# Turning x once and ordering the first projection block by hand in an SSD and attention trunk

## The chip, the core and the metric

The kernel runs on one core of a Trainium2 chip. The metric is the device time of one launch in microseconds. A core has TensorE (PE; the profile shows its weight loads apart, as PEld), VectorE (DVE), ScalarE (ACT), GpSimd (POOL) and SyncE (SP), which here only issues transfers. Each engine works through its own instructions in order; semaphores tie the engines together. ACT and POOL issue some transfers too, in order with their own work.

## The reference, cut to what matters

Sixteen meta tokens are put ahead of 1024 tokens of 1024 features; so L is 1040. Layer 0 is an SSD (Mamba-2) mixer and a gated FFN, layer 1 an attention and a gated FFN. The change lies at the very start of layer 0: the norm of the input, the first projections, and dt.

```python
def _rmsnorm(x, g):
    y = x32 * lax.rsqrt(jnp.mean(x32 * x32, axis=-1, keepdims=True) + NORM_EPS)
    return (y * g.astype(jnp.float32)).astype(x.dtype)

def _ssd_mixer(u, w_in, conv_w, conv_b, dt_bias, a_log, d_skip, gate_g, w_out):
    z, xbc, dt_raw = jnp.split(u @ w_in, [SSM_D_INNER, SSM_D_INNER + SSM_CONV_DIM], axis=-1)
    xbc = jax.nn.silu(_causal_dwconv(xbc, conv_w, conv_b))
    xs, b_in, c_in = jnp.split(xbc, [SSM_D_INNER, SSM_D_INNER + G * N], axis=-1)
    dt = jax.nn.softplus(dt_raw.astype(f32) + dt_bias.astype(f32))
    a = -jnp.exp(a_log.astype(f32))
...
    a_cs = jnp.cumsum(jnp.transpose(dt_c * a.reshape(G, E), (0, 3, 4, 1, 2)), axis=-1)
    decay_in = jnp.exp(jnp.where(causal, a_cs[..., :, None] - a_cs[..., None, :], -jnp.inf))
...
# per layer: h = h + mixer(rmsnorm(h)); h = h + ffn(rmsnorm(h))
```

## The kernel before

**Layout.** The stream h and the operands stand with features on the 128 partitions (eight tiles of 128 features, `KD = 8`) and tokens along the free axis. Tokens are cut into nine chunks of 116 (`CH`; the last has 112) and into three token tiles `TT` of 348, 348 and 344, three chunks each. x arrives with tokens on the partitions and has to be turned by PE, a 116 x 128 piece at a time, against the identity.

**Products.** A projection is made in three products of rounded numbers (`mm3`, lines 151 to 153): weights and operand are each split into a high part (a copy of ACT to the type fp32r) and a low part (the difference), and high x high, high x low and low x high are summed in PSUM. A block is 128 output features; for one token tile it takes 8 x 3 = 24 products (`project`). `load_w` fetches a block's weights on SP's queue, ACT makes the high part (line 144), POOL the low part (line 145).

**The start, `load_x`.** Nine chunks of x are fetched in turn on the queues of ACT and SP (`by_rows`, line 357). For each token tile j there are two steps, put in the order `ORD`:
- `stream(j)`: sums of squares of each token (line 318 on ACT, line 316 on DVE); for each k three turns (line 323), a copy to h (lines 326 and 328), and one fp32 product of `w_dt`, scaled by the norm's gain beforehand, with h for dt (line 329); then the token factors r (`token_rstd`, lines 202 to 208). For j = 2 each h is also spilled to memory (line 331).
- `scaled(j)`: x is multiplied by r in place, a token to a partition (line 340), turned a second time (line 345), and split with the gain into the operands `uh` and `ul` (lines 256 and 257).

**dt, `dt_path`.** A generator of three stages. The first takes the raw dt sums, turns them to tokens on partitions (line 403), multiplies by r (line 412), adds the bias and forms softplus. The second takes the running sums of dt*a within a chunk (lines 432 and 433). The third turns them back (line 445) and writes them to memory as `acs_d` and `ea_d` (line 451), from which the scan fetches them spread over partitions as D (line 567) and E (line 573).

**Group 0.** `mixer` then runs the six blocks of group 0 (`in_group`), each with three token tiles: project, a convolution of four taps (line 273 on ACT, three times line 276 on DVE), and silu (line 464), which `settle` leaves until the next convolution. A stage of `dt_path` is run after tiles 2, 5 and 8. PSUM gives the projections two banks (`mm`), and one more (`ex`) to each third tile. Then comes the scan of group 0, between whose steps the blocks of later groups are put; the scan's first products are lines 594 and 597, and its first DVE work on D is line 578.

**What sets the order.** Outside of `manual_schedule` the compiler's scheduler orders each engine's instructions after its own model of their times, and may put a later instruction ahead of an earlier one that isn't ready. Inside `manual_schedule` the instructions of PE, DVE, ACT and POOL keep the order of the program among themselves; others may still be put between them. SP's transfers are left to the scheduler. Before the change `load_x` and the six blocks of group 0 are ordered by the scheduler; the scan and all after it in the mixer by hand.

Of the kernel before, what the change touches and what calls it, by code (L numbers as in the profile page):

```python
# [8 lines left out]
F32 = mybir.dt.float32  # L9
# [4 lines left out]
P = 128  # L14
# [35 lines left out]
ORD = ((0, 0), (1, 0), (0, 1), (1, 1), (0, 2), (1, 2))  # L50
XB, SQD = 9, (1, 4, 7)
# [15 lines left out]
class Trunk:  # L67
    def __init__(self, ctx, tc, a):
# [10 lines left out]
        self.open = []  # L79
        self.consts()  # L80
# [198 lines left out]
    def load_x(self, pool, mx):  # L279
# [5 lines left out]
        wdt = self.wp.tile([P, 1024], F32, tag="w32", name="wdt")  # L285
        self.ln_exp()
        d = self.dp.tile([KD, P, L], F32, tag="h0_d", name="h0_d")
        r9 = mx.tile([P, 3, 3], F32, tag="r9", name="r9")
        dt = self.ex("dtr")
        xs = []  # L290
        for c, (t0, n) in enumerate(CH):
            xt = pool.tile([P, D], F32, tag="x", name=self.nm("x"), bufs=XB)
            if c == 0:
                nc.sync.dma_start(xt[:META, :], a["meta"])
                self.by_rows(nc.scalar, xt[META:n, :], a["x"][: n - META, :], n - META)
            else:
                self.by_rows(nc.sync if c % 2 else nc.scalar, xt[:n, :], a["x"][t0 - META : t0 - META + n, :], n)
            if c == 0:
# [3 lines left out]
            xs.append(xt)  # L302
        u = [(self.Q("uh", F32R), self.Q("ul", F32R)) for _ in range(KD)]
# [4 lines left out]
        def stream(j):  # L308
            s0, nn = TT[j]
            x3 = xs[3 * j : 3 * j + 3]  # L310
            for i in range(3):
                c = 3 * j + i
                n = CH[c][1]
                t = self.wp.tile([P, D], F32, tag="wl", name=self.nm("junk"))
                if c in SQD:
                    nc.vector.scalar_tensor_tensor(t[:n, :], x3[i][:n, :], 1.0, x3[i][:n, :], op0=ALU.mult, op1=ALU.mult, accum_out=ss[:n, c : c + 1])
                else:
                    nc.scalar.activation(t[:n, :], x3[i][:n, :], AF.Square, accum_out=ss[:n, c : c + 1])
            for k in range(KD):
                ps = self.lg("xT")  # L320
                for i in range(3):
                    n = CH[3 * j + i][1]
                    nc.tensor.transpose(ps[:, i * CB : i * CB + n], x3[i][:n, k * P : k * P + P], self.ident[:n, :n])
                h = hs[k][:, s0 : s0 + nn]
                if k % 2:
                    nc.scalar.activation(h, ps[:, :nn], AF.Copy)
                else:
                    nc.vector.tensor_copy(h, ps[:, :nn])
                nc.tensor.matmul(dt[j * H : j * H + H, :nn], wdt[:, k * H : k * H + H], h, start=k == 0, stop=k == KD - 1)
                if j == 2:  # L330
                    nc.sync.dma_start(d[k], hs[k][:, :L])
            self.token_rstd(ss[:, 3 * j : 3 * j + 3], CB, 3, y=r9[:, :, j])

        def scaled(j):
            s0, nn = TT[j]
            x3 = xs[3 * j : 3 * j + 3]
            for i, t in enumerate(x3):
                n = CH[3 * j + i][1]
                r = r9[:n, i : i + 1, j]
                nc.vector.tensor_scalar(t[:n, :], t[:n, :], r, None, op0=ALU.mult)  # L340
            for k in range(KD):
                ps = self.sm("xr")
                for i in range(3):
                    n = CH[3 * j + i][1]
                    nc.tensor.transpose(ps[:, i * CB : i * CB + n], x3[i][:n, k * P : k * P + P], self.ident[:n, :n])
                self.parts(ps[:, :nn], u[k], s0, nn, self.par("ssd_norm", k))

        for step, j in ORD:
            (scaled if step else stream)(j)
        return d, u, dt, r9  # L350
# [35 lines left out]
    def dt_path(self, ps, r9, cp):  # L386
# [10 lines left out]
        rows = self.tmp("rows")  # L397
        nc.gpsimd.memset(rows[:G, TT[2][1] : 3 * CB], 0.0)
        for j, (_, n) in enumerate(TT):
            nc.scalar.activation(rows[j * H : j * H + H, :n], ps[j * H : j * H + H, :n], AF.Copy)  # L400
        pv = self.sm("dt")
        for i in range(3):
            nc.tensor.transpose(pv[:CB, i * G : i * G + G], rows[:G, i * CB : i * CB + CB], self.ident[:G, :G])
# [1162 lines left out]
```

## Time and profile before

| | |
|---|---|
| runs | 3008.25, 3008.68, 3009.84 us; median 3008.68 |
| profiled execution | 3009.7 us, of which the span of the trace is 3008.0 |
| PE busy in the span | 2886.3 us (96%) |
| PE weight loads | 2776.1 us (92%) |
| DVE, ACT, POOL busy | 2304.7, 1653.0, 1306.0 us |
| fp32 dt products (line 329), first 138 us | 21.54 us busy |
| turns of line 323 and of line 345, first 138 us | 14.43 and 11.57 us busy |

A row of the order of time gives the start in us from the start of the span, the duration, engine, line, operation, what it writes and reads, the shapes and the count; in brackets the idle time of the engine ahead of it and what ended it. A row of the windows gives the busy time of each engine in that stretch and, after the count of its instructions, the granted PE clock (1.00 is full), the share of time in which the transfer engines were busy, and GB/s. A row of a line's or tile's instructions gives shortest, middle and longest duration in ns. An engine name with a q at its end (ACTq, SPq) marks the issuing of transfers, which isn't counted as busy.

### The profile page before, as it was taken

Reading aid. Unit: us, or ns where it says so; the run is one execution under the profiler, and the core shown is the slowest. Engines: PE = TensorE matmul, PEld = TensorE weight load, DVE = VectorE, ACT = ScalarE, POOL = GpSimd, SP = SyncE. Lnnn points to the kernel's source line nnn. Section 1 sums busy time; section 2 is a strip of 40 time slices with the busy share of each in tenths; the row PEclk is TensorE's granted clock in tenths of the full one; section 3 lists DMA queues with packets and bytes.
Section 4 is the critical chain, followed back from the end, with each engine's and each line's share of the span. In section 5 each row is a group of like instructions: output and inputs, shape, how many; then the busy total and the mean of one; then the engine's idle time right before and its main releaser. Section 6 shows DMA issues by size and latency. Waiting matters only on the chain. (4 is left out here: it accounts for less than half of the span.)

```text
span 3008.0 us, 58728 instructions
## 1 busy us (share of the span) xinstructions
PE 2886.3 (96%) x22535; PEld 2776.1 (92%) x22535; DVE 2304.7 (77%) x4062; ACT 1653.0 (55%) x3405; POOL 1306.0 (43%) x1257
## 2 busy tenths in 40 slices
PE   7999999989998999999999999999898999999998
PEld 4999898979998999999999999999798999999998
DVE  5587868886369788778976888888749788788875
ACT  4554545553145555555334888888636555555332
POOL 1254434442335666654433222222344666663441
PEclk9999999999999999999999999999999999999999
DMA  5233333323221222234132222221432222225231
GB/s 162 70 106 90 105 97 103 108 63 138 74 86 54 82 79 75 82 126 165 48 131 74 64 63 65 68 60 52 139 105 73 83 79 73 84 79 178 95 104 57
DMA packets 123465, 273.42 MB, mean 91 GB/s; under 512 B 13712, under 2 KB 53264, under 8 KB 123184
## 3 DMA queue, kind: packets, MB, share of 16 engines
q1 hardware_dynamic: 117808, 258.54, 27.8%
q10 hardware_dynamic: 4112, 6.56, 0.7%
q8 instruction: 177, 2.90, 0.4%
q0 software_dynamic: 1264, 4.57, 0.4%
q14 instruction: 104, 0.85, 0.1%
HBM read 201.25 MB, written 53.45 MB: 85 GB/s over the span
## 5 line engine op out<-in xcount | busy, mean ns | idle before, releaser
L151 PE MATMUL pj<-uh,wh 128*128 128x348 f32 (+2 forms) x1536 | 505.8, 329 | 11.8 <-ACT bk L609 6.0
L152 PE MATMUL pj<-ul,wh 128*128 128x348 f32 (+2 forms) x1536 | 499.1, 325 | 0.0
L153 PE MATMUL pj<-uh,wl 128*128 128x348 f32 (+2 forms) x1536 | 495.9, 323 | 0.0
L151 PE MATMUL p<-bh,fh 128*128 128x262 f32 x1408 | 404.3, 287 | 7.7 <-DVE c L276 5.6
L153 PE MATMUL p<-bh,fl 128*128 128x262 f32 x1408 | 403.7, 287 | 3.6 <-POOL fl L882 3.6
L152 PE MATMUL p<-bl,fh 128*128 128x262 f32 x1408 | 403.0, 286 | 0.0
L882 POOL TENSOR_TENSOR fl<-x,fh 128x1024 fp32r<-128x1024 f32 x88 | 212.4, 2415 | 274.4 <-ACT fh L881 178.1
L152 PE MATMUL p<-bl,wh 128*128 128x262 f32 x1056 | 302.7, 287 | 6.3 <-DVE bl L834 6.2
L151 PEld LDWEIGHTS pj<-uh,wh 128*128 128x128 f32 x1536 | 292.3, 190 | 15.6 <-ACT xbc L273 4.5
L151 PE MATMUL p<-bh,wh 128*128 128x262 f32 x1056 | 302.5, 287 | 0.9 <-ACT bh L833 0.9
L153 PE MATMUL p<-bh,wl 128*128 128x262 f32 x1056 | 302.2, 286 | 0.0
L276 DVE SCALAR_TENSOR_TENSOR c<-p,params,c 128x260 f32<-128x260 f32 x528 | 251.5, 483 | 57.2 <-ACT c L273 47.5
L152 PEld LDWEIGHTS pj<-ul,wh 128*128 128x128 f32 x1536 | 292.7, 191 | 1.7 <-issue 0.8
L153 PEld LDWEIGHTS pj<-uh,wl 128*128 128x128 f32 x1536 | 292.2, 190 | 0.8 <-issue 0.8
L145 POOL TENSOR_TENSOR wl<-w,wh 128x1024 fp32r<-128x1024 f32 (+2 forms) x76 | 154.6, 2036 | 314.0 <-ACT wh L144 314.0
L151 PEld LDWEIGHTS p<-bh,fh 128*128 128x128 f32 x1408 | 269.4, 192 | 8.6 <-ACT c L273 6.0
L153 PEld LDWEIGHTS p<-bh,fl 128*128 128x128 f32 x1408 | 269.7, 192 | 4.2 <-POOL fl L882 4.0
L152 PEld LDWEIGHTS p<-bl,fh 128*128 128x128 f32 x1408 | 269.6, 191 | 0.6 <-DVE bl L834 0.4
L152 PE MATMUL acc<-gl,wh 128*128 128x260 f32 x896 | 255.0, 286 | 12.8 <-DVE gl L1032 12.8
L151 PE MATMUL acc<-gh,wh 128*128 128x260 f32 x896 | 251.3, 285 | 7.8 <-DVE p L1077 7.7
L153 PE MATMUL acc<-gh,wl 128*128 128x260 f32 x896 | 253.8, 285 | 0.0
L923 DVE TENSOR_TENSOR c<-c,c 128x260 f32<-128x260 f32 x176 | 240.7, 1370 | 4.4 <-ACT c L919 1.4
(325 smaller groups left out, 8427.0 us busy)
## 6 DMA issues: line engine op xcount, KB each, us to landing
w<-in_w_up SPq DMA_DIRECT2D x88, 512.0 KB
g<-c SPq DMA_DIRECT2D x176, 130.0 KB
w<-in_w_down SPq DMA_DIRECT2D x44, 512.0 KB
w<-in_w_in SPq DMA_DIRECT2D x40, 512.0 KB
b<-g SPq DMA_DIRECT2D x32, 520.0 KB
E<-ea_d SPq DMA_DIRECT2D x32, 464.0 KB
D<-acs_d SPq DMA_DIRECT2D x32, 420.5 KB
h<-h_d SPq DMA_DIRECT2D x16, 520.0 KB
```

Of the source, the lines that this page charges most:

```text
L145: nc.gpsimd.tensor_tensor(wl[:, :n], w32[:, :n], wh[:, :n].bitcast(F32), op=ALU.subtract)
L151: mm(out, wh, uh, start=first, stop=False, skip_group_check=joins)
L152: mm(out, wh, ul, start=False, stop=False, skip_group_check=joins)
L153: mm(out, wl, uh, start=False, stop=last, skip_group_check=joins)
L276: nc.vector.scalar_tensor_tensor(out, ps[:, o + i : o + i + n], wcol(i), out, op0=ALU.mult, op1=ALU.add)
L882: tt(lo[:, :n], t, hi[:, :n].bitcast(F32), op=ALU.subtract)
L923: self.last_up = tt(g[:, :FN], g[:, :FN], v[:, :FN], op=ALU.mult)
```

## The change

x is turned once. The copy in h is scaled with features on partitions: the token factors of a token tile are put on a diagonal, and one fp32 product with a matrix of ones spreads them over all partitions (`factors` and its `spread`). `scaled(j, k)` multiplies the turned piece by the gain and the spread factors in one DVE instruction, and `operand(j, k)` splits the result. dt is no longer a product of fp32 weights with h: its weights are split into two parts that lie side by side, 32 + 32 columns for each k, and 16 products a token tile with `uh` and `ul` give 64 rows of sums. `dt_path` adds the halves as it turns them, by nine small products with two identities one above the other; its multiplication by r falls away.

The first block of group 0 is now run inside `load_x`, under `manual_schedule`: before each step k of its product, `project` calls a hook (`between`), which issues the turns, squares, factors, scalings and splits of the steps ahead, those of the next token tile too. dt's products follow each of the three tiles. The weights of block 1 are split at the end of the second tile. The first stage of `dt_path` is run right behind, and the other five blocks go on as before, ordered by the scheduler. Chunk 2 of x is fetched in two halves on both queues, and the weights of blocks 0 and 1 and `w_dt` are fetched between the chunks.

```diff
@@ project
         for k in range(kb):
             hi, lo = u[k]
+            if self.hook:
+                self.hook(k)
             self.mm3(...)
@@ load_x
-            if c == 0:
-                nc.sync.dma_start(wdt[:, : KD * H], a["w_dt"])
-                v = wdt[:, : KD * H].rearrange("p (k h) -> p k h", k=KD)
-                nc.gpsimd.tensor_tensor(v, v, self.par("ssd_norm", 0, KD).unsqueeze(2).to_broadcast([P, KD, H]), op=ALU.mult)
+        nc.sync.dma_start(xs[0][:META, :], a["meta"])
+        load(nc.scalar, 0, META)
+        load(nc.sync, 1)
+        load(nc.scalar, 2, 0, 64)
+        load(nc.sync, 2, 64)
+        load(nc.scalar, 3)
+        w0, wdt, w1 = w32(), w32(), w32()
+        nc.sync.dma_start(w0, blocks[0][0])
+        load(nc.sync, 5)
+        nc.sync.dma_start(wdt[:, : KD * H], a["w_dt"])
+        for c in (4, 6, 7, 8):
+            load(nc.sync if c == 7 else nc.scalar, c)
+        nc.sync.dma_start(w1, blocks[1][0])
...
+        def square(c):
...
+            if c % 3 == 1:
+                nc.vector.scalar_tensor_tensor(t[:n, :], xs[c][:n, :], 1.0, xs[c][:n, :], op0=ALU.mult, op1=ALU.mult, accum_out=ss[:n, c : c + 1])
+            else:
+                nc.scalar.activation(t[:n, :], xs[c][:n, :], AF.Square, accum_out=ss[:n, c : c + 1])
+        def turn(j, k):
+            s0, nn = TT[j]
+            ps = self.sm("xT")
             for i in range(3):
+                n = CH[3 * j + i][1]
+                nc.tensor.transpose(ps[:, i * CB : i * CB + n], xs[3 * j + i][:n, k * P : k * P + P], self.ident[:n, :n])
+            h = hs[k][:, s0 : s0 + nn]
+            if j or k % 2:
+                nc.scalar.activation(h, ps[:, :nn], AF.Copy)
+            else:
+                nc.vector.tensor_copy(h, ps[:, :nn])
+            if j == 2:
+                nc.sync.dma_start(d[k], hs[k][:, :L])
+            return ps[:, :nn] if j else h
+        def factors(j):
+            r = self.token_rstd(ss[:, 3 * j : 3 * j + 3], CB, 3, y=r9[:, :, j])
+            q = self.tmp("diag")
+            for i in range(3):
+                nc.vector.tensor_scalar(q[:CB, i * CB : i * CB + CB], self.ident[:CB, :CB], r[:CB, i : i + 1], None, op0=ALU.mult)
+            def spread():
+                ps = self.lg("rb")
+                nc.tensor.matmul(ps[:, : 3 * CB], self.ones[:CB, :], q[:CB, : 3 * CB], start=True, stop=True)
+                rb.append(self.tmp("rb"))
+                nc.scalar.activation(rb[j][:, : 3 * CB], ps[:, : 3 * CB], AF.Copy)
+            return spread
+        def scaled(j, k):
+            nn = TT[j][1]
+            src = turn(j, k) if j else hs[k][:, :nn]
+            t = self.tmp("x")[:, :nn]
+            nc.vector.scalar_tensor_tensor(t, src, self.par("ssd_norm", k), rb[j][:, :nn], op0=ALU.mult, op1=ALU.mult)
+            ts[j, k] = t
+        def operand(j, k):
+            s0, nn = TT[j]
+            self.parts(ts.pop((j, k)), u[k], s0, nn, None, nc.vector)
+        def between(j, k):
+            if j == 0 and k < 3:
+                turn(0, 5 + k)
+            if j < 2:
+                n = 3 * j + 3
+                if k < 3:
+                    square(n + k)
+                elif k == 3:
+                    later.append(factors(j + 1))
+                elif k == 4:
+                    later.pop()()
+            m = k + 3
+            if m < KD:
+                scaled(j, m)
+            elif j < 2:
+                scaled(j + 1, m - KD)
+            if m <= KD:
+                operand(j, m - 1)
+            elif j < 2:
+                operand(j + 1, m - KD - 1)
+            if j == 1 and k == KD - 1:
+                ws.append(parts(w1, D))
+        def dt(j):
+            s0, nn = TT[j]
+            ps = self.ex("dtr")
+            o = ps[: 2 * H, :nn]
+            w = both.rearrange("p (k m) -> p k m", k=KD)
             for k in range(KD):
+                for i, t in enumerate(u[k]):
+                    nc.tensor.matmul(o, w[:, k], t[:, HALO + s0 : HALO + s0 + nn], start=k + i == 0, stop=k + i == KD)
+            nc.scalar.activation(raw[: 2 * H, s0 : s0 + nn], o, AF.Copy)
+        for c in (1, 0, 2):
+            square(c)
...
+        for k in range(3):
+            turn(0, k)
+        spread = factors(0)
+        turn(0, 3)
+        spread()
+        turn(0, 4)
+        for k in range(3):
+            scaled(0, k)
+            if k == 0:
+                ws.append(parts(w0, D))
+            else:
+                operand(0, k - 1)
+        for j in range(3):
+            self.hook = lambda k: between(j, k)
+            blocks[0][1](ws[0], j)
+            self.hook = None
+            if j == 0:
+                both = self.wp.tile([P, 1024], F32R, tag="wh", name="wdts")[:, : 2 * KD * H]
+                b4, w3 = both.rearrange("p (k i h) -> p k i h", k=KD, i=2), wdt[:, : KD * H].rearrange("p (k h) -> p k h", k=KD)
+                nc.scalar.activation(b4[:, :, 0], w3, AF.Copy)
+                nc.vector.tensor_tensor(b4[:, :, 1], w3, b4[:, :, 0].bitcast(F32), op=ALU.subtract)
+            dt(j)
+        return d, raw, ws[1]
@@ dt_path
+        sums = cp.tile([P, H], F32, tag="sums", name="sums")
+        nc.vector.tensor_tensor(sums[: 2 * H], self.ident[: 2 * H, :H], self.ident[: 2 * H, H : 2 * H], op=ALU.add)
         pv = self.sm("dt")
-        for i in range(3):
-            nc.tensor.transpose(pv[:CB, i * G : i * G + G], rows[:G, i * CB : i * CB + CB], self.ident[:G, :G])
+        for j in range(3):
+            for i in range(3):
+                o = i * G + j * H
+                nc.tensor.matmul(pv[:CB, o : o + H], raw[: 2 * H, (3 * j + i) * CB : (3 * j + i) * CB + CB], sums[: 2 * H], start=True, stop=True)
...
-        tt(v3, pv[R].rearrange("p (c h) -> p c h", h=H), r9[:CB].rearrange("p i j -> p (i j)").unsqueeze(2).to_broadcast([CB, 9, H]), op=ALU.mult)
-        tt(v3, v3, bias, op=ALU.add)
+        tt(v3, pv[R].rearrange("p (c h) -> p c h", h=H), bias, op=ALU.add)
@@ in_block
-            ps = self.project(w, u, j, HALO, bank=self.ex if j == 2 else None)
+            ps = self.project(w, u, j, HALO, bank=self.ex if j == 2 and not self.hook else None)
@@ mixer
+            first = self.in_group(u := [], 0, rows[0])
+            with self.tc.manual_schedule(engines={E.PE, E.DVE, E.Activation, E.Pool}):
+                hd, dt, w1 = self.load_x(pool, first, u)
+            dt = self.dt_path(dt, mx)
+            next(dt)
...
-            for n, _ in enumerate(self.stream(into(0))):
+            for n, _ in enumerate(self.stream(first[1:], w1)):
                 if n % 3 == 2:
                     next(dt, None)
-                if n == 14:
+                if n == 11:
                     w0 = self.load_w(blocks[0][0], D)
```

More of the change, by code (lines that the diff above doesn't have):

```diff
@@ L276, in conv, with load_x @@
             nc.vector.scalar_tensor_tensor(out, ps[:, o + i : o + i + n], wcol(i), out, op0=ALU.mult, op1=ALU.add)
-    def load_x(self, pool, mx):
+    def load_x(self, pool, blocks, u):
         nc, a = self.nc, self.a
@@ L306, in load_x, with parts @@
         hs = [self.Q("h") for _ in range(KD)]
-        def stream(j):
+        def parts(w, n):
+            wh, wl = (self.wp.tile([P, 1024], F32R, tag=t, name=self.nm(t)) for t in ("wh", "wl"))
+            nc.scalar.activation(wh[:, :n], w[:, :n], AF.Copy)
+            nc.gpsimd.tensor_tensor(wl[:, :n], w[:, :n], wh[:, :n].bitcast(F32), op=ALU.subtract)
+            return wh, wl
+        def square(c):
+            n = CH[c][1]
+            t = self.wp.tile([P, D], F32, tag="wl", name=self.nm("junk"))
+            if c % 3 == 1:
+                nc.vector.scalar_tensor_tensor(t[:n, :], xs[c][:n, :], 1.0, xs[c][:n, :], op0=ALU.mult, op1=ALU.mult, accum_out=ss[:n, c : c + 1])
+            else:
+                nc.scalar.activation(t[:n, :], xs[c][:n, :], AF.Square, accum_out=ss[:n, c : c + 1])
@@ L319, in stream @@
-            for k in range(KD):
-                ps = self.lg("xT")
-                for i in range(3):
[L322 to L346, printed above, removed]
```

51 lines of the change are left out of this document (14 added, 37 removed).

## The prediction

> **What bounds the kernel now.** I read first the page, then the windows over the start, then the order of time of each engine in it. TensorE (PE) is busy almost everywhere, so a change at the start is worth what it moves the moment from which PE's order is the same before and after. That moment is the last product of the eighteenth tile of group 0 (six blocks, three tiles each); the first product of the scan, line 594, stands right behind it.
>
> ```profile
> span 3008.0 us, 58728 instructions
> ```
>
> ```profile
> core 0: us, PE busy (x) PEld busy (x) DVE busy (x) ACT busy (x) POOL busy (x), PEclk, DMA share, GB/s
> 0.00:17.80 17.80, 3.97 (x11) 1.53 (x11) 3.77 (x13) 3.79 (x7) 4.93 (x28) 1.00 0.92 236
> 17.80:31.80 14.00, 11.13 (x38) 3.87 (x38) 9.14 (x17) 8.59 (x21) 5.11 (x2) 1.00 0.52 148
> 31.80:36.00 4.20, 4.01 (x16) 1.84 (x16) 3.47 (x10) 1.43 (x3) 0.00 (x0) 0.70 0.42 125
> 36.00:83.50 47.50, 46.58 (x277) 34.72 (x275) 25.71 (x51) 28.05 (x49) 4.78 (x2) 0.99 0.31 114
> 83.50:99.00 15.50, 15.31 (x95) 15.34 (x96) 14.53 (x27) 6.55 (x12) 2.83 (x2) 1.00 0.20 64
> 99.00:116.00 17.00, 17.00 (x106) 16.46 (x104) 4.71 (x9) 11.25 (x15) 4.80 (x2) 1.00 0.38 94
> 116.00:120.20 4.20, 0.02 (x1) 0.01 (x1) 3.37 (x12) 3.07 (x4) 0.00 (x0) 0.83 0.97 242
> 120.20:125.60 5.40, 5.38 (x19) 5.40 (x20) 3.26 (x6) 3.01 (x5) 0.00 (x0) 0.50 0.29 100
> ```
>
> ```profile
> 36.07 0.64 PE L151 MATMUL pj<-uh,wh 128*128 128x352 f32 x1
> ...
> 138.13 0.36 PE L594 MATMUL cb<-xbc,xbc 128*116 128x116 f32 x2
> ```
>
> Before 36 us PE waits for x, for its squares and for the scaling. From 36 to 116 it is full: the scheduler mixes the turns and the dt products of the start with the tiles of blocks 0 and 1. In 83.5 to 99 there are only projections: 96 weight loads in 15.5 us, 0.161 us a product and 3.87 us a tile of 24. Then comes one hole:
>
> ```profile
> PE pj L151 <- DVE xbc L276: 5.0, 2, 4.2
> ```
>
> ```profile
> 116.76 1.60 DVE L578 TENSOR_SCALAR D<-D,cols 116x116 f32<-116x116 f32 x8 [9.04 <-DMA D<-acs_d]
> ```
>
> VectorE (DVE) had a scan instruction (L578) ordered ahead of convolutions and stood 9.04 us until D had landed; PE ran three tiles ahead, then stood 4.2 us, and did the next 20 products in 5.4 us at half the granted clock. At 0.161 they take 3.2, so the hole costs 4.2 + 2.2 = 6.4 us.
>
> **The change: what PE loses.** Removed are 24 fp32 dt products and 72 of the 144 turns.
>
> ```profile
> 39.73 0.46 PE L345 MATMUL xr<-ident,x 116*128 116x116 f32 x3
> 39.96 0.41 PE L152 MATMUL pj<-ul,wh 128*128 128x352 f32 x1
> ...
> 55.40 0.77 PE L329 MATMUL dtr<-h,wdt 128*32 128x344 f32 x2
> 56.10 0.52 PE L323 MATMUL xT<-ident,x 116*128 116x116 f32 x3
> 56.55 0.77 PE L329 MATMUL dtr<-h,wdt 128*32 128x344 f32 x2
> ```
>
> From start to start a dt product holds PE 0.70 us and three turns 0.23 to 0.45 (0.3 taken): 24 x 0.70 + 24 x 0.3 = 24.0 us. Added are 48 dt products of the form of a projection with 64 columns, whose cost the trace doesn't show; the moving side is the same 348, so I take 0.161 (7.7 us; 3.9 if half the columns were half the time), and three fp32 spreads by ones at 0.70 (2.1). PE's work falls by 14 us. If PE were full from its first product on, all of that would be gained; it isn't, for what follows.
>
> **The change: when the first tile begins.** ScalarE (ACT) issues half of x and computes nothing before its last issue.
>
> ```profile
> 0.83 14.35 ACTq L357 DMA_DIRECT2D x<-in_x  x9
> ...
> 16.34 1.04 ACT L318 ACTIVATE junk<-x 116x1024 f32<-116x1024 f32 x1
> ...
> 17.38 0.44 ACT L326 ACTIVATE h<-xT 128x348 f32<-128x348 f32 x1
> 17.72 1.04 ACT L318 ACTIVATE junk<-x 116x1024 f32<-116x1024 f32 x1
> ...
> 18.76 0.19 ACT L203 ACTIVATE r<-ss 116x3 f32<-116x3 f32 x1
> 18.99 0.21 ACT L204 ACTIVATE r<-r 116x3 f32<-116x3 f32 x1
> ```
>
> The new order keeps ACT's ten issues ahead of its work and puts a weight block (0.52 MB by its shape, 2.2 us at 236 GB/s) into SP's queue ahead of chunk 5; each queue gets about half of the bandwidth, so I put ACT's first square at 16.0 instead of 15.3 (bounds: 15.3, and 17.5 if all 2.2 fall on it). Behind ACT's issues queue its squares, copies, Ln and Exp, and for these wait DVE's factors, PE's spread and so every operand.
>
> ```profile
> 15.21 1.22 DVE L316 SCALAR_TENSOR_TENSOR junk<-x 116x1024 f32<-116x1024 f32 x1 [1.82 <-DMA x<-in_x]
> ...
> 19.23 0.16 DVE L205 TENSOR_TENSOR tb<-r 116x3 f32<-116x3 f32 x1 [1.55 <-ACT r L204]
> ...
> 19.82 0.16 DVE L208 TENSOR_TENSOR r<-r,tb 116x3 f32<-116x3 f32 x1
> ```
>
> ```profile
> 17.87 1.37 PE L329 MATMUL dtr<-h,wdt 128*32 128x348 f32 x2 [3.41 <-ACT h L326]
> ```
>
> ```profile
> 26.77 1.05 ACT L144 ACTIVATE wh<-w 128x1024 fp32r<-128x1024 f32 x1
> ```
>
> ```profile
> 39.86 2.37 POOL L145 TENSOR_TENSOR wl<-w,wh 128x1024 fp32r<-128x1024 f32 x1 [8.62 <-ACT wh L144]
> ```
>
> Two squares 2.1, a copy 0.4, Ln and Exp 0.5, DVE's four small steps 0.8, three diagonals at 0.2 (eight L578 take 1.60), the spread on a cold PE 1.4, its copy 0.4, the weights' high part 1.05: 16.0 + 7.3 = 23.3. The low part on GpSimd, 2.4 more, is needed by the third product: 25.7. PE has until then only 15 turns and the spread. So tile 0 begins near 25, some 11 us earlier than at 36.07.
>
> **The change: what paces the first block.** Between the products of a tile stand by hand the scaling, split and turn of operands three steps ahead, all in order on DVE and ACT.
>
> ```profile
> 33.80 1.54 DVE L257 SCALAR_TENSOR_TENSOR ul<-xr,params,uh 128x348 fp32r<-128x348 f32 x3
> ...
> 69.57 1.54 DVE L276 SCALAR_TENSOR_TENSOR xbc<-pj,params,xbc 128x348 f32<-128x348 f32 x3
> ```
>
> ```profile
> L254 DVE TENSOR_TENSOR ul<-h,uh x20: 508/516/1251, 1563.6 to 1609.1; 128x348 fp32r<-128x348 f32 x16, 128x344 fp32r<-128x344 f32 x4
> ```
>
> ```profile
> 50.83 0.65 ACT L273 ACTIVATE xbc<-pj,params 128x348 f32<-128x348 f32 x1
> ```
>
> DVE takes 0.49 for a scaling and about 0.46 for a low part (0.51 less the overlap that L257 shows). Tile 0 after 25: seven of each 6.7, a square 1.3, a copy 0.4, factors with their wait for ACT 2.0, and 0.2 at each of eight handovers: 12.0, to 37.5. PE needs there only 24 x 0.161 + 18 turns 1.8 + 0.7 = 6.4. Then PE waits in its own order: the dt weights are split behind the convolution (0.65 + 1.54 + 0.35), about 3 us; dt's 16 products take 2.6, or 4.6 at half clock, 3.6 taken: 44.1. Tile 1 has eight scalings and low parts 7.6, a square 1.3, factors 2.0, handovers 1.6: 12.5, to 56.6; dt 2.6; tile 2 with five scalings, six low parts, a convolution and 1 us of handovers 7.8, to 67.0; dt 2.6: **block 0 ends at 69.6**. PE has worked 27 of the 45 us. Bounds: 66 (ACT at 15.3, full clock, no handovers in tiles 1 and 2), 79 (ACT at 17.5, slow parts).
>
> **From there to the mark.** Fifteen tiles at 3.87 are 58.05. The dt path adds nine small products that the trace doesn't show (0.1 each, the price of a turn; 0 to 2 in all), sums and rows between tiles, together 3.1. That is 130.7, before any hole. D: the chain dt, acs, rows, D is the same, still left to the scheduler, begins right behind block 0, and goes past the same SP queue:
>
> ```profile
> 109.50 0.70 SPq L567 DMA_DIRECT2D D<-acs_d  x2
> ```
>
> Landing took 7.3 us after that issue. Nothing moves L578 behind the convolutions, so I expect the wait again. It is worth 0 if it is ordered later and 6.4 if it is the same; I take the 4.2 of the wait alone, since the lost clock depends on where the hole falls. Sum: 69.6 + 58.05 + 3.1 + 4.2 = 135.0 against 138.1, a gain of 3.1. The profiled execution took 3009.7 us (1.7 outside its span); 1.0 above the median of the runs, 3008.7. So 3009.7 - 3.1 = 3006.6, less that 1.0: **about 3006 us**. The spill of h, eight transfers on SP's queue, comes some 8 us later than before; nothing in group 0 reads it, and the fifteen tiles of work that are still to come hide it, so I cost it at nothing; if a weight block waits behind it, that is 2.2 us a block. The removed rescaling of x frees DVE, which PE's later tiles don't wait for: nothing.
>
> **Rivals.**
> (1) The hole closes and block 0 runs at its lower bound: 66 + 58.05 + 3.1 = 127.2, 10.9 less, 2998 us. For it: PE's work really is 14 us less, and the scheduler may pull tiles of block 1 into PE's waits. Against it: block 1's weights are split only at the end of tile 1.
> (2) Half clock in block 0, the slower side. The clock falls after a stretch in which PE was busy less than half:
>
> ```profile
> 26.62:30.04 3.42, 2.58 (x13) 1.04 (x11) 3.42 (x2) 1.67 (x3) 3.42 (x2) 1.00 0.19 19
> 30.04:33.45 3.41, 1.46 (x10) 1.04 (x11) 3.34 (x8) 0.59 (x2) 1.20 (x1) 1.00 0.66 205
> 33.45:36.86 3.41, 3.41 (x9) 1.32 (x8) 1.89 (x4) 1.27 (x3) 0.00 (x0) 0.50 0.20 83
> ```
>
> 2.58 of 3.42 keeps it, 1.46 of 3.41 loses it. Tile 0 has 6.4 of 12.0 by my count, just above. Where it falls below, PE's 27 us become up to 50, tiles 0 and 1 take some 15.5 instead of 12, the three dt rounds 4.6: block 0 ends near 81, and 81 + 65.35 = 146.4, 8.3 more: 3017 us. It decides from a share under one half. Against it: a slow PE is a busy PE, and regains the clock. The Trainium skill, in "TensorE: Matmul & The Clock Gate", Part 4: PE-mode transpose, says that turns don't count as busy for the gate; by that tile 0 would count only 3.9 + 0.7 of 12.0, and this rival would be the rule. No window of this trace holds turns alone.
> (3) The change doesn't do what it says: the scheduler fills the hand order with later work and what was removed was hidden anyway: 3009 us.
>
> **How the numbers follow.** Forecast 0.42, rival (1) 0.35, (2) 0.17, (3) 0.06. About 0.2% (6 us) is what a measurement can tell from no change: faster than 3002.7 is rival (1) and a twentieth of the forecast's side, 0.39; slower than 3014.7 is (2) and a little, 0.20; the rest 0.41. The forecast's own range, from 0 and 6.4 for the hole and 2 us either way in block 0, is 3000 to 3011; the range over the cases is 2995 to 3017.
>
> **What would show it.** First product near 25 us and 24 of them spread over some 12 us, with PE waiting for DVE: the pacing. Block 0's last product near 67. Line for the scan's first product at 135 (127 for rival 1, 146 for 2). A DVE wait for D of some 9 us: the hole stays. Granted clock 0.5 between 25 and 70: rival (2). I'm wrong at the root if PE is full in block 0, or if another engine's wait stands in the fifteen tiles.

## The result, and the profile after

| | before | after |
|---|---|---|
| median of 20 runs each | 3009.4 us | 3011.8 us |
| lowest and highest | 3005.7, 3014.9 | 3003.9, 3020.6 |
| profiled execution, its span | 3009.7, 3008.0 us | 3013.2, 3011.5 us |
| first projection product | 36.07 us | 26.21 us |
| mark (first product of the scan) | 138.13 us | 139.63 us |

The ratio of the times is 1.0004, with a 95% interval from 0.9997 to 1.0011: no difference that these runs can tell. The forecast was "about 3006 us", with a chance of 0.41 for a time within 6 us, about 0.2%, of before, and of 0.39 for a time shorter than that. The page of the kernel after, its span and PE's share:

```profile
span 3011.5 us, 58666 instructions
PE 2878.9 (96%) x22484; PEld 2783.4 (92%) x22484; DVE 2311.5 (77%) x4079; ACT 1653.8 (55%) x3417; POOL 1309.0 (43%) x1256
```

PE's busy time fell by 7.4 us (2886.3 before) and the span didn't follow. Where it went is seen in the windows of the kernel after, cut at the steps of the prediction: ACT's first square, the first product, the last product of tile 0, the first and the last dt product behind it, the last product of tile 1, the last dt product of all, the hole, the mark.

```profile
core 0: us, PE busy (x) PEld busy (x) DVE busy (x) ACT busy (x) POOL busy (x), PEclk, DMA share, GB/s
0.00:18.07 18.07, 3.05 (x12) 2.19 (x12) 2.80 (x11) 1.29 (x2) 5.21 (x27) 1.00 0.92 229
18.07:26.21 8.14, 2.69 (x9) 1.74 (x9) 3.08 (x11) 5.08 (x11) 0.68 (x1) 1.00 0.76 198
26.21:42.66 16.45, 11.79 (x41) 9.43 (x41) 13.14 (x29) 8.35 (x21) 1.66 (x1) 1.00 0.10 32
42.66:45.81 3.15, 0.00 (x1) 0.00 (x0) 3.02 (x7) 1.22 (x4) 0.00 (x0) 0.86 0.00 0
45.81:50.51 4.70, 4.70 (x16) 3.67 (x17) 0.00 (x0) 0.00 (x0) 0.00 (x0) 0.50 0.38 117
50.51:63.97 13.46, 9.79 (x50) 8.03 (x49) 8.49 (x23) 8.98 (x23) 0.00 (x0) 0.83 0.03 13
63.97:80.70 16.73, 16.37 (x110) 15.06 (x110) 11.14 (x23) 11.87 (x23) 3.67 (x2) 1.00 0.75 277
80.70:121.40 40.70, 40.70 (x255) 40.08 (x253) 22.64 (x45) 25.95 (x36) 11.16 (x6) 1.00 0.34 96
121.40:127.78 6.38, 3.81 (x25) 3.64 (x24) 4.29 (x11) 4.10 (x6) 0.00 (x0) 1.00 0.36 119
127.78:139.63 11.85, 11.85 (x75) 11.85 (x75) 6.95 (x12) 4.34 (x9) 0.00 (x0) 1.00 0.12 45
```

PE begins 10 us sooner than before, then spends 37.8 us (26.21 to 63.97) on two tiles and one round of dt. In tile 0 and tile 1 (the rows of 26.21 and 50.51) it has gaps, and DVE works for 13.14 of 16.45 us and 8.49 of 13.46; in the row of dt(0) (45.81) it is the other way round: PE is full, and DVE and ACT do nothing. The rows of the order of time that show the steps:

```profile
0.83 17.13 ACTq L437 DMA_DIRECT2D x<-in_x  x10
...
11.38 2.19 PE L331 MATMUL xT<-ident,x 116*128 116x116 f32 x10 [3.01 <-DMA x<-in_x]
...
18.07 1.06 ACT L323 ACTIVATE junk<-x 116x1024 f32<-116x1024 f32 x1 [15.98 <-DMA x<-in_x]
...
25.06 3.19 DVE L361 SCALAR_TENSOR_TENSOR x<-h,params,rb 128x348 f32<-128x348 f32 x2
25.53 2.35 POOL L314 TENSOR_TENSOR wl<-w,wh 128x1024 fp32r<-128x1024 f32 x1 [19.14 <-ACT wh L313]
...
28.74 0.66 PE L151 MATMUL pj<-ul,wh 128*128 128x352 f32 x1 [1.87 <-DVE ul L253]
...
45.81 0.55 PE L400 MATMUL dtr<-uh,wdts 128*64 128x348 f32 x1 [3.15 <-DVE wdts L428]
46.16 0.49 PE L400 MATMUL dtr<-ul,wdts 128*64 128x348 f32 x1
46.45 0.49 PE L400 MATMUL dtr<-uh,wdts 128*64 128x348 f32 x1
...
52.68 0.58 DVE L361 SCALAR_TENSOR_TENSOR x<-xT,params,rb 128x348 f32<-128x348 f32 x1 [6.92 <-ACT h L334]
...
120.71 1.61 DVE L658 TENSOR_SCALAR D<-D,cols 116x116 f32<-116x116 f32 x8 [5.97 <-DMA D<-acs_d]
...
124.17 0.40 PE L150 MATMUL pj<-uh,wh 128*128 128x348 f32 x1 [2.58 <-DVE xbc L277]
...
139.63 0.36 PE L674 MATMUL cb<-xbc,xbc 128*116 128x116 f32 x2
```

ACT comes to its first square at 18.07. The first two scalings of DVE take 3.19 us, while those after them take 0.57 each, and end 0.4 us behind POOL's subtraction (27.88); ACT starts on the result of the first at 25.66, so it is the second that is held. The second product waits for it. PE waits 3.15 us for dt's weights, then does dt(0) at 0.29 us a product (half clock), and the turn that DVE needs next stands behind that in PE's order, so DVE waits 6.92. That wait has a second part: it ends with ACT's copy of the turned piece to h (52.21 to 52.65), and ACT, in order, first copies dt's sums and makes a square, 1.4 us together (50.81 to 52.21). Last comes the hole: DVE waits 5.97 us for D.

### The profile page after: what moved, and what is told of

It is laid out like the page before. It is cut to its first block, busy times and chain, and to the rows that moved or that the text cites. A ratio compares the mean times of both kernels' runs of the same rounds, so it can differ in the third digit from the quotient of the medians.

```text
span 3011.5 us, 58666 instructions
## 1 busy us (share of the span) xinstructions
PE 2878.9 (96%) x22484; PEld 2783.4 (92%) x22484; DVE 2311.5 (77%) x4079; ACT 1653.8 (55%) x3417; POOL 1309.0 (43%) x1256
```

## The experiments

All times are of runs beside the kernel before on the same chip, as a ratio to it with its 95% interval. The marks are from one profiled execution of each. "Tile 1" is where PE comes to the weights of the 48th projection product, which ends some 0.5 us later. By hand this is the last product of the second tile, and in runs 3, 8 and 10 its last but one. In before and run 5 it is no end of a tile, since the scheduler has put products of block 1 among the first 48 (in before, the second tile's last operand is begun at 62.20). As a measure of what a mark of one execution is good for: the kernel after and runs 1, 4, 6 and 7, whose start up to the first product is nearly the same, have it between 25.72 and 26.43.

| kernel | first product | tile 1 | mark | ratio to before |
|---|---|---|---|---|
| before | 36.07 | 61.48 | 138.13 | 1 |
| after | 26.21 | 63.97 | 139.63 | 1.0004 [0.9997, 1.0011] |
| 1 dt behind tile 2 | 25.72 | 56.85 | 149.81 | 1.0045 [1.0033, 1.0058] |
| 2 two chunks issued by SP | 19.89 | 58.90 | 136.63 | 0.9986 [0.9977, 0.9995] |
| 3 scheduler's order | 31.49 | 53.36 | 131.56 | 0.9975 [0.9964, 0.9986] |
| 4 after, D tied | 25.92 | 64.71 | 137.57 | 0.9989 [0.9980, 0.9998] |
| 5 before, D tied | 36.49 | 61.67 | 131.43 | 0.9979 [0.9969, 0.9989] |
| 6 block 0's weights early | 26.39 | 62.16 | 140.64 | 0.9992 [0.9982, 1.0003] |
| 7 dt's weights early | 26.43 | 60.86 | 138.14 | 0.9993 [0.9984, 1.0002] |
| 8 scheduler, D tied | 31.28 | 52.39 | 125.87 | 0.9962 [0.9950, 0.9975] |
| 9 hand order, 2 + 4 + 6 + 7 | 24.56 | 55.64 | 128.49 | 0.9964 [0.9950, 0.9977] |
| 10 scheduler, 2 + 4 | 28.45 | 51.52 | 123.06 | 0.9949 [0.9937, 0.9960] |
| 11 as 9, dt inside the tiles | 25.48 | 53.72 | 130.79 | 0.9974 [0.9964, 0.9983] |
| 12 hand order, 2 + 4 + 7 | 19.52 | 52.60 | 125.46 | 0.9950 [0.9936, 0.9963] |

What follows the mark is the same program in the versions from after, but it isn't equally long in their profiled executions: from the mark to the end of the span 2867.5 us (run 4) to 2873.8 (run 2). So marks tell where time went at the start, and the ratios what it is worth, to some us.

**1. dt's rounds all behind tile 2.**

```diff
-            dt(j)
+        for j in range(3):
+            dt(j)
```

> The changed kernel with the three rounds of dt products moved behind the third tile of block 0; nothing is left out. Theory (block 0 is paced by what stands in order in it): PE's wait of 3.15 us for the dt weights and DVE's wait of 6.92 us for a turn queued behind the first dt round both go, and the first scan product, at 139.6 us in the changed kernel, comes at 132 to 135. Rival (PE's own work paces block 0): the products are as many as before, so the mark stays within 1 us of 139.6. Second rival (the wait for D in the fifteen tiles takes up what is gained): block 0 ends 5 us earlier and the mark moves by less than 2.

The first half of it came true: both waits went, and tile 1 ended 7 us sooner. But the mark was 10 us later, where 132 to 135 was expected. The windows of this run, and two rows of its order of time:

```profile
40.00:90.50 50.50, 42.39 (x240) 37.33 (x239) 26.76 (x60) 27.41 (x59) 4.75 (x2) 0.88 0.32 116
90.50:126.50 36.00, 32.61 (x201) 31.54 (x200) 21.50 (x39) 21.63 (x31) 9.80 (x5) 1.00 0.22 62
126.50:138.00 11.50, 5.90 (x23) 5.93 (x24) 4.22 (x13) 5.98 (x7) 0.00 (x0) 0.70 0.63 167
```

```profile
130.62 0.85 DVE L659 TENSOR_SCALAR D<-D,cols 116x116 f32<-116x116 f32 x4 [6.56 <-issue]
...
132.10 0.63 PE L150 MATMUL pj<-uh,wh 128*128 128x348 f32 x1 [6.51 <-DVE xbc L277]
```

dt's sums were last complete at 88 us instead of 81, the path from dt to D followed, and D's first DVE instruction came at 130.62 instead of 120.71. PE, already ahead, stood 6.5 us and then lost its clock (0.70). So dt's place in block 0 isn't a cost that can be pushed back: it is the head of the chain that ends in D.

**2. Chunks 6 and 8 of x issued by SP.**

```diff
-            load(nc.sync if c == 7 else nc.scalar, c)
+            load(nc.scalar if c == 4 else nc.sync, c)
```

> The changed kernel with chunks 6 and 8 of x issued by SP instead of ACT. Theory (ACT's own transfer issues hold its first square back, to 18.07 us in the changed kernel): ACT's last issue comes at about 10.4, its first square at 11 to 12, the first product at 20 to 22 instead of 26.2, and the mark 4 to 6 us earlier than 139.6. Rival (x itself lands too late): the first square still waits for its chunk, and the first product moves by less than 2 us.

The order of time of this run:

```profile
11.57 1.06 ACT L323 ACTIVATE junk<-x 116x1024 f32<-116x1024 f32 x1 [9.48 <-DMA x<-in_x]
...
19.89 0.66 PE L150 MATMUL pj<-uh,wh 128*128 128x352 f32 x1 [1.04 <-ACT uh L252]
```

ACT's first square and the first product come 6.5 and 6.3 us sooner: ACT's issues, not the data, were what held tile 0 back. In the kernel after, too, the data were there: PE was turning pieces of all three chunks of tile 0 from 11.38 us on, and ACT's first square came at 18.07. Only 3.0 us of it reach the mark, where 4 to 6 were expected; PE's stand before its fifteenth tile grew (3.10 us of waiting, then half clock).

**3. The same block, left to the scheduler.**

```diff
-            with self.tc.manual_schedule(engines={E.PE, E.DVE, E.Activation, E.Pool}):
-                hd, dt, w1 = self.load_x(pool, first, u)
+            hd, dt, w1 = self.load_x(pool, first, u)
```

> The changed kernel without the hand order of the first block: the same instructions, ordered by the scheduler. Theory (the hand order leaves PE waiting in block 0, since it lets nothing of block 1 in before the end of the second tile): the scheduler moves turns ahead of dt products and fills waits, and the mark comes at 134 to 138 instead of 139.6. Rival (the hand order is what makes the new form no slower): the mark comes at 142 to 150, since the scheduler's model has the operands ready too early.

Nothing is computed otherwise, PE begins 5 us later than by hand, and the mark is 8.1 us sooner, 6.6 sooner than before. 131.56 is below the 134 to 138 of the theory. So the change without its order by hand is worth something, and the order by hand takes it back.

**4 and 5. D tied behind the fifteenth tile's convolution**, in the kernel after and in the kernel before: the first of D's eight DVE instructions may not be put ahead of that convolution's last.

```diff
+            if g + c + i == 0:
+                self.tc.add_manual_dep(ins.ins, self.convs[14].ins.name, nosync, reason="behind a convolution")
```

> The changed kernel with the first scan instruction on D (line 578 of the kernel before) tied on DVE behind the convolution of the fifteenth tile of group 0, which is issued after D has landed. Theory (DVE's wait of 5.97 us for D costs PE its wait of 2.58 us): the mark comes at 136.5 to 137.5 instead of 139.6. Rival (PE is held by other work there): it stays at 139 to 140. Third possibility: the scan's first step is late by the moved instruction, and what is gained at the mark is lost within 20 us behind it.

> The kernel before with one tie: the first vector instruction of D may not be put ahead of the fifteenth tile's convolution; nothing is computed otherwise. In the trace of before the vector engine reached D at 116.76 us and waited 9.04 us for its transfer, the projections behind it began 4.2 us late and then ran 5.4 us at half clock; the mark (the first product of the scan) stood at 138.13. Theory (the hole is a wait that hand placement takes out whole, 4.2 us of waiting and some 2.2 us of half clock): mark 131.5 to 132.5, ratio 0.9976 to 0.9985 to before. Rival (the wait moves to the next thing that hangs on D): mark 136 to 138, ratio 0.9993 to 1.0003. If the theory holds, the hole was the same size in the kernel before, so it can't explain why the change gained nothing.

DVE's rows for D have no wait left, in run 4 and in run 5:

```profile
128.62 1.60 DVE L660 TENSOR_SCALAR D<-D,cols 116x116 f32<-116x116 f32 x8
```

```profile
122.48 1.60 DVE L580 TENSOR_SCALAR D<-D,cols 116x116 f32<-116x116 f32 x8
```

and from 85 us to the mark the view of PE's waits shows none in either run. The hole was worth 6.7 us of mark before (138.13 to 131.43; the theory had 131.5 to 132.5), and 2.1 after (137.57, 0.07 above what was expected). These two runs take the mask off: without a hole on either side the change makes the start 6.1 us longer (131.43 to 137.57). The ratios, 0.9979 and 0.9989, point the same way, but by some 3 us and with intervals that overlap, so the size rests on the two marks. The hole had hidden three quarters of that, since tiles that come late stand less in front of a late D.

**6. Block 0's weights split ahead of the factors**, the high part on DVE.

```diff
+        nc.vector.tensor_copy(w0h, w0)
+        nc.gpsimd.tensor_tensor(w0l, w0, w0h.bitcast(F32), op=ALU.subtract)
+        ws.append((w0h, w0l))
         spread = factors(0)
```

> The changed kernel with the first block's weights split ahead of the first factors: the high part by the vector engine instead of the scalar engine, the low part by GpSimd behind it, while both wait for the sums of squares. Theory (GpSimd's 2.35 us subtraction beside the vector engine's two scalings is what stretched these to 3.19 us, against 0.57 each elsewhere, and the second product waited 1.87 us for it): the two scalings take 1.1 to 1.3 us, the second product follows the first within 0.8 us, tile 0 ends 1.0 to 2.5 us sooner after its own first product, mark 137.1 to 138.6 against 139.6, ratio 0.9996 to 1.0003 to before. Rival (the scalings are slow for another reason, or the weights' landing comes so late that the copy holds the factors up): scalings still near 3 us or first product later than 26.2, mark 139 to 141.

The two scalings took 1.06 us in place of 3.19 and tile 0 was 2.0 us shorter (26.39 to 40.80 for 26.21 to 42.66), so POOL's subtraction was what stretched them. The first product came at 26.39, just behind the 26.2 of the rival, and the mark was outside what the theory expected and in the range of the rival: 140.64, since the fifteenth tile, the one with the hole, took 9.5 us instead of the 6.7 of the kernel after.

**7. dt's weights split inside tile 0**, at its third step.

```diff
+            if j == 0 and k == 2:
+                both = ...
+                nc.scalar.activation(b4[:, :, 0], w3, AF.Copy)
+                nc.vector.tensor_tensor(b4[:, :, 1], w3, b4[:, :, 0].bitcast(F32), op=ALU.subtract)
```

> The changed kernel with dt's weights split inside tile 0 (at its third step) instead of behind it. In the changed kernel the tensor engine waited 3.15 us for them at 42.66 us, then ran dt's 16 products at 0.29 us each at half clock, and the vector engine waited 6.92 us for the turn behind them. Theory (that wait is what cost block 0 its time, and the half clock follows from it): no wait for the weights over 0.7 us, the 16 products in 2.6 to 3.2 us, tile 1 ends 3.5 to 6 us sooner than 63.97, mark 134 to 136.5 against 139.6, ratio 0.9982 to 0.9993 to before. Rival (the tensor engine would wait there anyway, for the operands of tile 1 that the vector engine has still to make): the wait moves to the first products of tile 1, half clock stays, tile 1 ends 62 to 64, mark 138 to 140.

PE didn't wait for them, dt(0) ran at full clock, and DVE's longest wait fell from 6.92 to 1.91 us:

```profile
43.68 0.32 PE L406 MATMUL dtr<-uh,wdts 128*64 128x348 f32 x1
43.84 0.32 PE L406 MATMUL dtr<-ul,wdts 128*64 128x348 f32 x1
...
48.35 0.58 DVE L361 SCALAR_TENSOR_TENSOR x<-xT,params,rb 128x348 f32<-128x348 f32 x1 [1.91 <-ACT h L334]
```

So the half clock there followed from the wait. Tile 0 itself became 1 us longer (26.43 to 43.84). Tile 1 ended 3.1 us sooner, short of the 3.5 to 6 expected, and the hole took half of that: 138.14, not 134 to 136.5.

**8. Runs 3 and 4 together.**

> The changed kernel with the first block's order left to the scheduler (as in the third run) and D tied behind the fifteenth tile's convolution (as in the fourth). The third run's mark was 131.56 with 3.5 us of its own hole between tiles 13 and 14, and the fourth run's tie was worth 2.1 us. Theory (the two are independent): mark 127.5 to 129, ratio 0.9955 to 0.9972 to before, which beats both kernels. Rival (the tie makes the scheduler lay the tiles out otherwise, or the wait for D only moves): mark 131 to 133, ratio 0.9972 to 0.9985.

125.87, below what was expected, and 0.9962 of before. Against run 5 (before, tied) the mark is 5.6 us sooner, and the median of the runs, taken on the same chip, 5.5 us shorter (2999.1 and 3004.6): this is what the change is worth without its order by hand. The new order of the transfers is in it; x turned once and dt from the operands were not tried apart. Against run 4 (hand order, tied) it is 11.7 us sooner. Its windows, cut at about its 24th, 48th, 72nd and 96th projection product:

```profile
31.28:43.21 11.93, 9.86 (x49) 8.26 (x50) 9.34 (x29) 5.20 (x12) 0.00 (x0) 1.00 0.14 45
43.21:52.39 9.18, 9.18 (x66) 8.49 (x65) 9.18 (x23) 7.77 (x19) 0.00 (x0) 1.00 0.29 119
52.39:61.84 9.45, 8.58 (x60) 7.53 (x59) 7.58 (x17) 7.04 (x16) 0.00 (x0) 1.00 0.85 340
61.84:66.46 4.62, 4.62 (x32) 4.51 (x30) 0.00 (x0) 1.01 (x2) 0.00 (x0) 1.00 0.00 0
```

All nine squares, and many turns, had been put ahead of the first product, where ACT and DVE had little else to do, and dt's products stand between the projections. So from 43.21 to 52.39 PE and DVE are full at once, and ACT at 85%. By hand the squares and factors of tiles 1 and 2 stand inside tiles 0 and 1, and dt in one piece between tiles, and the engines wait for one another more: the first 48 products take 37.8 us in the kernel after and 21.1 in run 8.

**9, 12 and 11. Can the hand order be mended?** Run 9 puts the mends of 2, 4, 6 and 7 together; 12 leaves out 6; 11 takes run 9 and puts dt's products for tiles 0 and 1 at the fourth step of the next tile (`if j and k == 3: dt(j - 1)`).

> The changed kernel with its order by hand kept, and all that the earlier runs found mended together: chunks 6 and 8 issued by SP, the first block's weights split ahead of the factors, dt's weights split inside tile 0, D tied behind the fifteenth tile's convolution. With the tie alone the mark stood at 137.57 and with the tie and the scheduler's order at 125.87. Theory (the hand order lost by three waits of its own, for the issue, the weights and dt's weights, whose shares of 6.3 us at the first product, 1.7 us at the end of tile 0 and 2 to 3 us at the end of tile 1 add up once D no longer sets the end): mark 125.5 to 128.5, ratio 0.9955 to 0.9970 to before. Rival (the order itself is the cost: tile 1 alternates one engine at a time, whatever the first tile does): mark 129 to 133, ratio 0.9970 to 0.9985.

> The run with all mended and the hand order, without the early split of the first block's weights: three mends (issue, dt's weights, tie). With that split the vector engine stood until 16.34 us for the weights to land, and its next operation but one, of 116x3, took 1.86 us beside GpSimd's subtraction, so the first product came at 24.56; without it, with the issue mended alone, at 19.89. Theory (the early split is a loss once the squares come early): first product 19.5 to 20.5, tile 1 ends 53.5 to 55 against 55.64, mark 126 to 127.7 against 128.49, ratio 0.9955 to 0.9968 to before. Rival (tile 0 waits for the split wherever it stands): tile 1 ends 55.5 to 56.5, mark 128.3 to 129.5.

> As the run with all mended and the hand order, but dt's 16 products of tiles 0 and 1 stand inside the next tile, at its fourth step, instead of ahead of it (those of tile 2 stay behind tile 2). Theory (16 products in one piece ahead of tile 1 hold back the turns that the vector engine needs, and with them tile 1's operands: it waited 5.4 us for such turns when dt's weights were early): mark 1 to 4 us below the run with all mended, vector engine's wait for the turns between tiles 0 and 1 under 2.5 us. Rival (the vector and scalar engines set tile 1's length, at some 11 us of vector work for 8 operands, and the place of dt is indifferent): mark within 1 us of it.

Run 9 reached the upper end of what was expected, and its first product came 4.7 us later than in run 2. Its order of time shows why:

```profile
16.34 0.69 DVE L419 CAST wh<-w 128x1024 fp32r<-128x1024 f32 x1 [2.92 <-DMA w<-in_w_in]
17.12 2.34 POOL L420 TENSOR_TENSOR wl<-w,wh 128x1024 fp32r<-128x1024 f32 x1 [10.74 <-DVE ss L202]
17.62 1.86 DVE L205 TENSOR_TENSOR tb<-r 116x3 f32<-116x3 f32 x1 [0.51 <-ACT r L204]
```

DVE, in order, stood until the weights had landed, and then a step of 3 elements to a partition took 1.86 us, until POOL was done. Without mend 6 (run 12) the first product came at 19.52, where it was expected, and tile 1's end at 52.60 and the mark at 125.46 were better than that. The hand order, with three mends, is thus as good as the scheduler's with the tie alone, and 14.2 us ahead of the one it is made from. It gets there another way: its first 48 products still take 33.1 us, where run 8 takes 21.1, but they begin 11.8 us earlier. Run 11 ended tile 1 1.9 us sooner than run 9, but its mark was 2.3 us later, not 1 to 4 sooner: its theory fell. Its last dt product started at 76.13 us (72.23 in run 9), and PE waited 1.4 us for a convolution at 90.94, where run 9 has no such wait; whether the one follows from the other isn't shown.

**10. The scheduler's order with both mends, 2 and 4.**

> The changed kernel with the scheduler's order, D tied, and chunks 6 and 8 issued by SP. With the scheduler's order the scalar engine still stood from 7.3 to 17.1 us in its transfer issues, and the first product came at 31.28. Theory (the issues hold up the squares there too): first square of the second kind by 12 us, first product 24 to 28, mark 119.5 to 123.5 against 125.87, ratio 0.9937 to 0.9957 to before. Rival (the transfers themselves, which run at 215 to 290 GB/s from 4 to 21 us, set it; or the tiles behind wait for weights): first product 29 to 31, mark 124.5 to 126, ratio 0.9955 to 0.9970.

The mark of 123.06 and the ratio lie in the theory's ranges; the first product at 28.45 is just outside: ACT's last square, which waited for its chunk until 25.38, had been ordered ahead of ACT's copy of the spread factors (26.43). Runs 10 and 12 are the best measured here, half a per cent below both kernels; their intervals don't tell them apart.

## Why the prediction was right in its number, by its own steps

| step | predicted | measured |
|---|---|---|
| ACT's first square | 16.0 (15.3 to 17.5) | 18.07 |
| first product | near 25 | 26.21 |
| tile 0 | 12.0 us | 16.45 |
| wait for dt's weights | about 3 | 3.15 |
| dt(0) | 3.6 (2.6 or 4.6) | 4.70 |
| tile 1 | 12.5 | 13.46, to where its last product comes up |
| block 0 ends | 69.6 (66 to 79) | 80.70, of which one tile of block 1 (3.87) and the first of dt's turns (1.4) stand ahead of it: 75.4 |
| from there to the mark | 65.4 | 64.2 |
| mark | 135.0 | 139.63 |

- **What PE loses.** The 48 dt products cost 0.155 to 0.16 us each at full clock, as taken; that half the columns would be half the time, the other bound, is wrong. The nine small products of dt's turn cost more than the 0.1 each that was put: 12 records, six products, took 1.4 us. PE's own work did fall; of the 14 us counted, runs 5 and 8 show a gain of 5.6 for the whole change without its order by hand.
- **First tile.** The mechanism, ten issues ahead of ACT's work, was right, and shown by run 2. The term was 2 us too small: the bound took the queue's bandwidth, but ACT's last issue came only at 17.64, though a single one takes about 0.3 us. In the trace's records each of ACT's issues from the fifth on waits for a semaphore that an earlier transfer had used, the last one for that of a transfer issued at 7.84; that ACT stood until those transfers had landed is read from this and was not tried apart.
- **The pace of block 0.** It was right that DVE and ACT pace it and PE waits. Tile 0 is the term that was mis-sized, by 4.4 us. Two of them are the scalings held up by POOL, which the sum didn't have (run 6: tile 0 2.0 shorter without). The Trainium skill, in "SBUF — State Buffer", Who interferes with whom, has that rule: a DVE instruction with two inputs in SBUF contends with a GpSimd instruction that reads SBUF, over a pair of ports that one of them has to itself. The trace agrees, with 3.19 us for two scalings and 1.86 for a step of 3 elements. What is left of the 4.4 was not separated; PE's half clock, below, is likely part of it.
- **The wait for dt's weights** was costed rightly (3 and 3.15). What was missing is what stood behind it: the half clock that followed and DVE's 6.92 us behind dt(0).
- **The hole.** "I expect the wait again" was right, and it was 2.6 us of PE's time, not 4.2. The runs show a sharper thing than the prediction had: while D sets the end, what tiles gain or lose is partly swallowed (runs 2, 6, 7). That is how a start that is 6.1 us worse with the hole tied became 1.5 us worse without.
- **Rival (2), half clock in block 0,** was true in its condition, and the forecast wrong to put it aside; but at the start the clock hadn't fallen, it hadn't yet risen. PE did run at half clock for some 25 of block 0's 54.5 us (26.21 to 41.5, 44.9 to 51.7, 58.6 to 62.0). Its price, a block 0 that ends near 81, was too high against the 75.4. PE was at half clock for less than half of the time, and DVE and ACT set part of the pace whatever the clock is; how much each counts wasn't separated. The forecast stood on a full clock in tile 0, and that step failed: products followed one another there at 0.29 us, not 0.161.
- **Rival (1)** failed on both its conditions. **Rival (3)** gives nearly the time, 3009, but by another way: what was removed was not hidden, it was given back by the order.
- **A slip in the sum:** 25 and 12.0 are 37.0, and the sum goes on from 37.5. It changes nothing of the above.

So the call of no difference and the range over the cases held by the size of the errors, and not because the sum was right. The two errors in the mark, 5.8 us too little for block 0 and 1.2 too much behind it, come to 0.15% of the time, and any mark within some 6 us of before would have been no difference. That is luck in part, at a chance of 0.41 against 0.39 for faster. The forecast's own range, up to 3011, was missed by 0.8 us, and the gain of 3 us it named is not there. The steps that failed are the pace of tile 0 (12.0 us, measured 16.45) and the full clock that it stood on.

## What to carry to other kernels

When a change takes work out and adds an order by hand, measure the two apart: here the one gave 5.6 us and the other cost 11.7 by the marks (some 8 by the ratios), and with a wait behind it that swallowed part of both the sum looked like nothing. Close a known wait behind the change before judging it, since a wait for a transfer can swallow both gain and loss. In an order by hand, look for an engine that issues transfers and computes, for a one-off preparation that the next product needs, and for a block of one engine's work that stands ahead of what another engine waits for.

## What the runs showed of the hardware

**The clock column can't be read at the start.** In the windows of the kernel after, PEclk is 1.00 up to 41 us; but in its order of time the products follow one another at 0.29 to 0.30 us until 41.5, and at about 0.16 from there on:

```profile
39.78 0.49 PE L151 MATMUL pj<-ul,wh 128*128 128x352 f32 x1
40.08 0.49 PE L152 MATMUL pj<-uh,wl 128*128 128x352 f32 x1
40.37 0.78 PE L331 MATMUL xT<-ident,x 116*128 116x116 f32 x3
...
42.17 0.32 PE L151 MATMUL pj<-ul,wh 128*128 128x352 f32 x1
42.34 0.32 PE L152 MATMUL pj<-uh,wl 128*128 128x352 f32 x1
```

So PE was at half clock from its first product on, with no record of it: the column seems to know only of changes.

**Gaining the clock takes more than keeping it.** The clock changes in steps of 3.41 us: in the column it falls at about 44.9, rises at 51.7, falls at 58.6 and rises at 62.0. These windows have that length and are cut some 0.1 us behind the changes, first PE alone, then two with all engines:

```profile
27.97:31.38 3.41, 2.64 (x11) 1.00 0.49 154
31.38:34.79 3.41, 2.52 (x8) 1.00 0.00 0
34.79:38.20 3.41, 1.51 (x3) 1.00 0.00 0
38.20:41.61 3.41, 3.41 (x16) 1.00 0.00 0
41.61:45.03 3.42, 1.05 (x8) 0.98 0.00 0
45.03:48.44 3.41, 2.63 (x9) 0.50 0.45 135
```

```profile
55.27:58.68 3.41, 0.59 (x2) 0.30 (x2) 2.70 (x12) 1.64 (x5) 0.00 (x0) 0.98 0.00 0
58.68:62.10 3.42, 3.26 (x12) 2.60 (x12) 1.64 (x5) 1.31 (x3) 0.00 (x0) 0.52 0.00 0
```

Full clock came after windows with 3.41 and 3.26 us busy, and not after 2.64, 2.52 or 2.63; it was lost after 1.05 and 0.59. In the kernel before, 2.58 of 3.42 kept it. The prediction's "busy less than half" was a rule for losing it, and it was used for a PE that hadn't gained it yet.

The Trainium skill's rule that turns don't count as busy ("TensorE: Matmul & The Clock Gate", Part 4: PE-mode transpose), which the prediction weighed, can't be decided by this trace. Tile 0 did run at half clock until 41.5, as that rule would have it; but the windows ahead of it were short of the 3.26 with all their turns counted. Line 331's turns take 1.56 of the 3.41 us in the window that gained the clock (38.20 to 41.61). Without them 1.85 are left by subtraction, but 2.91 by the records of the projection products alone, since records overlap and the ends of matmuls are modelled; the 2.63 that weren't enough (45.03 to 48.44, without a turn) lie between the two.
